# State-space scan chunks moved from beside the z projection into attention, with z through DRAM and the chunk results kept in SBUF

## The chip, the cores and the metric

The kernel runs on one core of a Trainium2 chip. The metric is the device time of one execution in microseconds (us). TensorE is PE in the profile's rows (PEld are its weight loads), VectorE is DVE, ScalarE is ACT, GpSimd is POOL and SyncE is SP. Each engine works through its own instructions in a fixed order; an instruction that waits holds up everything behind it on its engine. Loads are issued from SP's queue, nearly all stores from ACT's queue. L179 means line 179 of the kernel's file; after the change most line numbers behind 570 differ.

## The reference

Two layers over 256 context and 1024 latent tokens of width 1024. Each layer is a mixer and a SwiGLU feed-forward block, both with norms and a modulation. What matters here is the mixer's two halves, which share an input and an output projection:

```python
q, k, v, z, xbc, dt = split(h @ w_in)            # one projection
attn = softmax(q k^T / 8) v                      # 8 query heads, 2 key heads of 64
xs, B, C = split(silu(conv(xbc)))                # 8 state-space heads of 64, state 128
for direction in (forward, backward):            # chunks of 128 tokens
    scores  = (C B^T) * decay                    # inside a chunk
    y      += scores @ (xs*dt) + (C @ h_in) * exp(acum)   # h_in: state before the chunk
y   = rmsnorm((y + d_skip * xs) * silu(z)) * ssd_norm
out = concat(attn, y) @ w_out
```

Context tokens get an output in the first layer only, so layer 0 has ten tiles of 128 tokens in its mixer's output and layer 1 has eight. Context queries see the 256 context keys, latent queries all 1280.

## The kernel before, in words

Matmuls in reduced form (`fp32r`) take every operand as a high and a low part, and `mm3` (L177 to 181) does a product as three of them. `split` (L109 to 111) makes the two parts: ACT copies the high one, DVE (or POOL) subtracts to get the low one. A tile of 128 tokens is the unit of nearly everything.

A layer's mixer has these stages. The convolution's projection; `kv`; `q`, beside which `ssd_states` runs the state recurrence over the chunks and writes each chunk's incoming state `h_d` to DRAM; then `z`, and beside it the scan chunks; then attention with the output projection; then the feed-forward block. `w_tok` (L360) is the loop over tiles of the projections: 24 matmuls of 512 columns a tile for q and z, then the tile's evaluation, then a `filler`, which is one step of another stage's generator. This is how two stages are put beside each other: the order in which the program emits instructions sets priorities, and the framework's list scheduler then fixes each engine's order from it.

One scan chunk (`ssd`, L629) has three parts. `decays` builds a 128 x 1024 decay matrix for each direction: a select on POOL (L639), four broadcast matmuls (L644) and four scans on DVE (L648), and a sum on POOL (L649). `chunk` multiplies C with B (L664) and C with the states of both directions (L668), multiplies the decays with the first on DVE (L670) and multiplies that with the inputs (L674), eight heads of 64 columns. `finish` adds the parts (L681 to 685), multiplies with the gate (L686), norms (L688), transposes on PE (L691), splits, and stores the result to DRAM (`mix_d`, L694). Chunk inputs come from DRAM by three loads (L656 to 658). `gate` (L701) leaves silu(z) in one of eight small SBUF buffers (`s2`, 128 x 512). Four buffers `L` hold the decays of two chunks.

`attention` (L748) works in units of one tile, one key head and two of its query heads, four units a tile. `scores` multiplies q with k (L785), scales with the running minimum on DVE (L786), takes the exponential on ACT (L792), and normalizes on POOL (L794), into one of six probability buffers; it runs two units ahead of `values`, which transposes probabilities on PE (L807), splits them (L110, L111) into one of two, later three, buffers, and multiplies with v (L814). After the fourth unit of a tile `oproj` multiplies the tile before with `w_out` (48 matmuls of 512 columns); half of its input comes from attention, half is loaded again from `mix_d` (L833). `attention` is a generator, too: its first units run beside the last chunks, and it gets its third split buffer and the last two `w_out` tiles only when the chunks' memory is free (L1019). PSUM has five banks of kind `w` and three of kind `s`.

The pools that bind are `x` (six buffers of 128 x 1024: chunk inputs and states, q of even tiles, the output norm), `s2` (eight), `raw` (two: weights before the split, q of odd tiles) and a ring of five split weight tiles that `pump` fills in a planned order, z's units before `w_out`'s.

## Time and profile before

| | us |
|---|---|
| runs shown: median of 3 (lowest, highest) | 3388.87 (3368.36, 3391.09) |
| profiled execution: its own time | 3388.8 |
| its span, first to last instruction | 3387.1 |
| layer 0: first z matmul to first output projection | 343.3 to 554.9 |
| layer 0: steady attention, five tiles | 635.9 to 832.4 |
| layer 1: first z matmul to first output projection | 2149.6 to 2373.4 |
| layer 1: steady attention, four tiles | 2412.2 to 2569.3 |
| mean granted TensorE clock | 0.965 of full |

How to read it: the page gives busy time of each engine and, in 40 equal slices, its tenths; a busy PE includes time in which a matmul waits inside the engine's pipeline. A window's row gives the same for a stretch that the reader chooses, with the granted clock. A row in order of time begins with its start and its length; in square brackets stands how long the engine had been idle and what ended that. A group's row gives count, total busy time, mean ns of one, and idle time ahead of it by what ended it.

### The profile page before, as it was taken

Reading aid. Unit: us, or ns where it says so; the run is one execution under the profiler, and the core shown is the slowest. Engines: PE = TensorE matmul, PEld = TensorE weight load, DVE = VectorE, ACT = ScalarE, POOL = GpSimd, SP = SyncE. Lnnn points to the kernel's source line nnn. Section 1 sums busy time; section 2 is a strip of 40 time slices with the busy share of each in tenths; the row PEclk is TensorE's granted clock in tenths of the full one; section 3 lists DMA queues with packets and bytes.
Section 4 is the critical chain, followed back from the end, with each engine's and each line's share of the span. In section 5 each row is a group of like instructions: output and inputs, shape, how many; then the busy total and the mean of one; then the engine's idle time right before and its main releaser. Section 6 shows DMA issues by size and latency. Waiting matters only on the chain.

```text
span 3387.1 us, 44081 instructions
## 1 busy us (share of the span) xinstructions
PE 3151.0 (93%) x16599; PEld 2601.6 (77%) x16599; DVE 1833.4 (54%) x3298; ACT 1231.2 (36%) x2332; POOL 1364.4 (40%) x1267
## 2 busy tenths in 40 slices
PE   6899967999899999988999999887999999999997
PEld 4677656888777888876777788666888788888886
DVE  2557876666534334436334557887666344444446
ACT  4433236666632121134222343236666411111112
POOL 4327434544533223236344534744544421212213
PEclk8899888999999999999999999888999999999999
DMA  6276533211333222135444325632112311111113
GB/s 219 77 223 209 176 125 114 80 63 66 108 119 113 88 88 75 57 106 169 137 143 131 125 70 164 227 131 79 69 69 82 100 49 45 57 38 56 45 49 112
DMA packets 283981, 360.00 MB, mean 106 GB/s; under 512 B 18160, under 2 KB 212176, under 8 KB 283512
## 3 DMA queue, kind: packets, MB, share of 16 engines
q1 hardware_dynamic: 237768, 291.71, 27.5%
q10 hardware_dynamic: 46000, 65.47, 5.3%
q8 instruction: 131, 2.15, 0.3%
q14 instruction: 82, 0.67, 0.1%
HBM read 291.61 MB, written 65.52 MB: 105 GB/s over the span
## 4 chain that ended last, share of the span: by engine, by line
PE 43%; DVE 3%; DMA 3%; POOL 2%; issue 2%; ACT 1%; ACTq 0%; POOLq 0%; DVEq 0%; SPq 0%
PE ps_w L179 7%; PE ps_w L180 7%; PE ps_w L181 7%; PE ps_s L179 4%; PE ps_s L181 4%; PE ps_s L180 4%; PE ps_w L814 2%; PE ps_w L807 2%; PE ps_s L785 2%; DMA xt<-in_norm_mix_post 1%; POOL w_t L111 1%; PE ps_w L230 0%; DVE xt L411 0%; POOL rstd_t L187 0%; DMA raw_t<-in_w_in 0%
## 5 line engine op out<-in xcount | busy, mean ns | idle before, releaser
L111 POOL TENSOR_TENSOR w_t<-raw_t,w_t 128x1024 fp32r<-128x1024 f32 (+1 forms) x220 | 546.7, 2488 | 1238.9 <-ACT w_t L110 1230.0
L929 DVE TENSOR_TENSOR ffn_acc<-ffn_acc,ps_s 128x512 f32<-128x512 f32 x560 | 380.2, 686 | 371.5 <-PE ps_s L181 369.7
L110 ACT CAST w_t<-raw_t 128x1024 fp32r<-128x1024 f32 (+1 forms) x248 | 256.7, 1037 | 669.4 <-PE ps_w L181 233.7
L179 PE MATMUL ps_s<-w_t,xt 128*128 128x512 f32 x792 | 315.0, 398 | 18.8 <-DVE ffn_acc L929 7.7
L181 PE MATMUL ps_s<-w_t,xt 128*128 128x512 f32 x792 | 308.8, 392 | 2.5 <-DVE xt L111 2.5
L180 PE MATMUL ps_s<-w_t,xt 128*128 128x512 f32 x792 | 310.0, 391 | 0.0
L910 DVE TENSOR_TENSOR s2t<-s2t,ps_w 128x512 f32<-128x512 f32 (+1 forms) x110 | 69.7, 634 | 439.9 <-PE ps_w L181 439.7
L786 DVE TENSOR_SCALAR_CACHE_REDUCE att_a<-ps_s 128x512 f32<-128x512 f32 (+1 forms) x400 | 227.4, 587 | 144.4 <-PE ps_s L785 131.1
L179 PE MATMUL ps_w<-hb,w_t 128*128 128x512 f32 x704 | 276.4, 393 | 3.5 <-ACT s2t L333 2.6
L179 PE MATMUL ps_w<-ha,w_t 128*128 128x512 f32 x704 | 275.0, 392 | 1.8 <-POOL ha L337 1.8
L181 PE MATMUL ps_w<-hb,w_t 128*128 128x512 f32 x704 | 275.5, 391 | 0.0
L180 PE MATMUL ps_w<-hb,w_t 128*128 128x512 f32 x704 | 275.3, 391 | 0.0
L180 PE MATMUL ps_w<-ha,w_t 128*128 128x512 f32 x704 | 275.2, 391 | 0.0
L181 PE MATMUL ps_w<-ha,w_t 128*128 128x512 f32 x704 | 274.9, 391 | 0.0
L794 POOL TENSOR_SCALAR att_a<-att_a,att_st 128x1280 f32<-128x1280 f32 (+1 forms) x144 | 181.8, 1265 | 163.2 <-DVE att_st L793 93.1
L110 ACT CAST xt<-s2t 128x512 fp32r<-128x512 f32 (+2 forms) x148 | 80.4, 543 | 423.4 <-DVE s2t L910 351.9
L807 PE MATMUL ps_w<-cst_all,att_a 128*128 128x128 f32 x1312 | 199.7, 278 | 0.8 <-issue 0.8
L792 ACT ACTIVATE att_a<-att_a,att_st 128x1280 f32<-128x1280 f32 (+1 forms) x144 | 183.0, 1272 | 36.5 <-DVE att_st L791 29.4
L179 PEld LDWEIGHTS ps_s<-w_t,xt 128*128 128x128 f32 x792 | 149.4, 189 | 60.5 <-issue 9.7
L111 DVE TENSOR_TENSOR xt<-s2t,xt 128x512 fp32r<-128x512 f32 (+2 forms) x148 | 167.9, 1134 | 39.3 <-ACT xt L110 37.5
L181 PEld LDWEIGHTS ps_s<-w_t,xt 128*128 128x128 f32 x792 | 148.8, 188 | 36.7 <-DVE xt L111 3.8
L180 PEld LDWEIGHTS ps_s<-w_t,xt 128*128 128x128 f32 x792 | 149.6, 189 | 26.5 <-issue 0.4
(268 smaller groups left out, 7338.3 us busy)
## 6 DMA issues: line engine op xcount, KB each, us to landing
raw_m<-in_w_mod SPq DMA_DIRECT2D x80, 512.0 KB
raw_t<-in_w_gate SPq DMA_DIRECT2D x66, 512.0 KB
raw_t<-in_w_up SPq DMA_DIRECT2D x66, 512.0 KB
raw_t<-in_w_down SPq DMA_DIRECT2D x66, 512.0 KB
xt<-xs SPq DMA_DIRECT2D x44, 512.0 KB
raw_t<-in_w_in SPq DMA_DIRECT2D x32, 512.0 KB
xs<-xt ACTq DMA_DIRECT2D x28, 512.0 KB
ssd_x<-xtok SPq DMA_DIRECT2D x36, 384.0 KB
```

The lines of the kernel that those rows point to most:

```text
L110: self.nc.scalar.copy(hi, src)
L111: (eng or self.nc.vector).tensor_tensor(lo, src, hi.bitcast(F32), op=ALU.subtract)
L179: mm(out, st[0], mv[0], start=first, stop=False)
L180: mm(out, st[0], mv[1], start=False, stop=False)
L181: mm(out, st[1], mv[0], start=False, stop=last)
L785: nc.tensor.matmul(s[:, :m], qs[t][c][:, hd], kst[:, g, j:j + m], start=c == 0, stop=c == 1)
L786: nc.vector.tensor_scalar(pb[:, j:j + m], s[:, :m], -0.125, None, op0=ALU.mult, op1=ALU.min, accum_out=st[:, n:n + 1])
L792: nc.scalar.activation(pb, pb, AF.Exp, bias=nmx, scale=-1.0, accum_out=st[:, 4:5])
L794: nc.gpsimd.tensor_scalar(pb, pb, st[:, 5:6], 1.0, op0=ALU.mult, op1=ALU.mult)
L807: nc.tensor.transpose(tp[:, (2 * k + h) * P:(2 * k + h + 1) * P], pr[h][:, (k2 + k) * P:(k2 + k + 1) * P], self.ident)
L910: nc.vector.tensor_tensor(s, s, ps["u"][:, :n], op=ALU.mult)
L929: nc.vector.tensor_tensor(acc[t][:, s], acc[t][:, s], p, op=ALU.add)
```

## The change

The z stage no longer has a filler. `gate` sends silu(z) to a new DRAM tensor `z_d`, and `mix_d` is gone. The scan is driven from the loop over attention's units: three steps a tile, one after each of the first three units, so that chunk t is computed in the units of tile t (`chunk`; load and decays of the next; `finish`). Its result stays as two `s2` buffers (`mix`) until `oproj` of that tile, at the end of the next tile. There is one pair of decay buffers, of which one lies in attention's large buffer `ha`, so that five probability buffers are left; `scores` is called for one head before and one head after `values`. The three split buffers and all of `w_out` are laid out from the start; the last three `w_out` tiles are loaded at the beginning of attention. The additions in `chunk` and `finish` are ordered so that PSUM is left earlier. The constant masks are loaded where `ssd_prep` needs them instead of at the program's start, and the state recurrence has a pool of its own that closes before z.

```diff
-        c = self.cst.tile([P, 6 * P + 2 * NT], F32, name="cst_all")
...
+        c = self.cst.tile([P, P + 2 * NT], F32, name="cst_id")
...
-        self.mix_d = [d(f"mix{l}", [NT, P, 1024]) for l in range(DEPTH)]
+        self.z_d = [d(f"z{l}", [NT, P, 512]) for l in range(DEPTH)]
...
+        mk = self.x(n=5 * P)
+        nc.sync.dma_start(mk, self.I["cst"][:, P:6 * P])
...
+    def gate(self, l, t, p):
+        z = self.s2()
+        self.nc.scalar.activation(z, p, AF.Silu)
+        self.nc.scalar.dma_start(self.z_d[l][t], z)
...
+        def load(c):
+            bx, hin, z = self.x(), self.x().rearrange("p (d n) -> p d n", d=2), self.s2()
...
+            nc.sync.dma_start(z, self.z_d[l][c])
+            ins[c] = bc, hin, xt, z
...
-            L = [lp.tile([P, 1024], F32, tag="L", bufs=4, name="ssd_L") for d in range(2)]
...
-            pi = [self.psw(), self.psw()]
+            ys = []
             for d in range(2):
+                pi = self.psw()
                 for g in range(2):
...
+                y = self.s2()
+                nc.vector.tensor_tensor(v8(y), v8(pi), hb8(self.ex[:, 0, d, c]), op=ALU.mult)
+                ys.append(y)
...
             nc.vector.tensor_tensor(y2, y2, y, op=ALU.add)
+            nc.vector.tensor_tensor(y2, y2, py, op=ALU.add)
+            mid[c] = y, y2, xt, z
...
-            self.split(y2.bitcast(F32R), y.bitcast(F32R), pt)
-            for i, half in enumerate((y2, y)):
-                nc.scalar.dma_start(self.mix_d[l][c, :, i * 512:(i + 1) * 512], half)
...
+            hi, lo = self.s2(F32R), self.s2(F32R)
+            self.split(hi, lo, pt)
+            mix[c] = hi, lo
...
         def steps():
-            for i in range(len(cs) + 1):
...
+            load(cs[0])
+            decays(cs[0])
+            yield
+            for i, c in enumerate(cs):
+                chunk(c)
+                yield
                 if i + 1 < len(cs):
...
+                    load(cs[i + 1])
+                    decays(cs[i + 1])
                 yield
...
+                finish(c)
+                yield
...
-        pbuf = [ha[:, i * TOK:(i + 1) * TOK] for i in range(6)]
+        NPB = 5
+        pbuf = [ha[:, i * TOK:(i + 1) * TOK] for i in range(NPB)]
...
+        L = [lp.tile([P, 1024], F32, name="ssd_L"), ha[:, NPB * TOK:NPB * TOK + 1024]]
+        mix = {}
+        scan = self.ssd(l, L, ha[:, NPB * TOK + 1024:NPB * TOK + 1536], mix)
...
-            ms = self.x()
-            nc.sync.dma_start(ms, self.mix_d[l][t])
-            ms = ms.bitcast(F32R).rearrange("p (s k n) -> p k s n", s=2, k=4)
+            hi, lo = (a.rearrange("p (k n) -> p k n", k=4) for a in mix.pop(t))
...
+        next(scan)
         for i, u in enumerate(units):
             if i + 2 < len(units):
-                scores(units[i + 2])
+                scores(units[i + 2], (0,))
...
             values(u)
...
-            if i % 4 == 3 and i > 3:
+            if i + 2 < len(units):
+                scores(units[i + 2], (1,))
+            if i % 4 < 3:
+                next(scan, None)
+            elif i > 3:
                 oproj(tiles[i // 4 - 1])
...
-                k.w_tok(l, "z", 512, qt, gate, zfill)
-                att = k.attention(l, early)
...
+                k.w_tok(l, "z", 512, qt, lambda t, p: k.gate(l, t, p), lambda: k.load_q(l, qt[0]) if next(nz) == len(qt) - 3 else None)
...
+                with tc.tile_pool(name=f"att{l}", bufs=1, reuse_waits="tile") as atp:
+                    k.attention(l, kv, atp, early)
```

What this does to the engines' orders shows in three places. PE within layer 0's z stage, before (L179 to L181 are z, the rest a scan chunk):

```order
L180 MATMUL ps_s<-w_t,ha 128x512
L181 MATMUL ps_s<-w_t,ha 128x512
L668 MATMUL ps_w<-xt 128x256 x4
L179 MATMUL ps_s<-w_t,ha 128x512
L180 MATMUL ps_s<-w_t,ha 128x512
L181 MATMUL ps_s<-w_t,ha 128x512
L674 MATMUL ps_w<-xt,ssd_L 128x64 x8
L179 MATMUL ps_s<-w_t,ha 128x512
L180 MATMUL ps_s<-w_t,ha 128x512
L181 MATMUL ps_s<-w_t,ha 128x512
L664 MATMUL ps_s<-xt 128x128 x2
```

PE at the end of layer 0's z stage, now (L809 are scores, L830 transposes, L837 values; L661, L673, L678 are the decays' and the chunk's matmuls):

```order
L179 MATMUL ps_s<-w_t,hb 128x512
L180 MATMUL ps_s<-w_t,hb 128x512
L181 MATMUL ps_s<-w_t,hb 128x512
L809 MATMUL ps_s<-att_c,xt 128x256 x4
L661 MATMUL ps_w<-eaT,pick 128x512 x4
L809 MATMUL ps_s<-att_c,xt 128x256 x8
L673 MATMUL ps_s<-xt 128x128 x2
L809 MATMUL ps_s<-att_c,xt 128x256 x2
L830 MATMUL ps_w<-cst_id,att_a 128x128 x4
L809 MATMUL ps_s<-att_c,xt 128x256 x2
L837 MATMUL ps_w<-att_c,att_b 128x256
L678 MATMUL ps_w<-xt 128x256 x4
```

Here z's matmuls end in one run, 179 of them without another instruction between, and the first chunk stands behind the first scores.

DVE in a steady tile of layer 0's attention, before (L786 are score evictions, L111 splits, L791 and L793 the softmax's small steps):

```order
L793 RECIPROCAL att_st<-att_st 128x1
L786 TENSOR_SCALAR att_a,att_st<-ps_s 128x512
L111 TENSOR_TENSOR att_pt<-ps_w,att_pt 128x512
L111 TENSOR_TENSOR att_b<-ps_w,att_b 128x512
L786 TENSOR_SCALAR att_a,att_st<-ps_s 128x256
L111 TENSOR_TENSOR att_c<-ps_w,att_c 128x512
L786 TENSOR_SCALAR att_a,att_st<-ps_s 128x512 x2
```

And now (L810 are the evictions; L665 the scans, L698 the gate's product, L700 the norm):

```order
L665 SCALAR_TENSOR_TENSOR ssd_L<-ps_w,ssd_L 128x512
L810 TENSOR_SCALAR att_a,att_st<-ps_s 128x512
L111 TENSOR_TENSOR att_c<-ps_w,att_c 128x512
L665 SCALAR_TENSOR_TENSOR ssd_L<-ps_w,ssd_L 128x512
L810 TENSOR_SCALAR att_a,att_st<-ps_s 128x256
L698 TENSOR_TENSOR s2t<-s2t 128x512
L815 TENSOR_REDUCE att_st<-att_st 128x1
L665 SCALAR_TENSOR_TENSOR att_a<-ps_w,att_a 128x512 x2
L815 TENSOR_REDUCE att_st<-att_st 128x1
L111 TENSOR_TENSOR att_pt<-ps_w,att_pt 128x512
L810 TENSOR_SCALAR att_a,att_st<-ps_s 128x512
L700 SCALAR_TENSOR_TENSOR s2t<-s2t,rstd_t,att_a 128x512
```

The chunk's DVE work now stands between the evictions and splits that PE waits for.

SP's queue around the load of v in layer 0, now (L121 and L780 are `w_out` tiles, L768 is v, L651 z, L751 q, L648 a chunk's B and C):

```order
L640 DMA att_a<-in_ssd_norm 128x512
L121 DMA raw_t<-in_w_out 128x1024 x2
L768 DMA att_b<-v_108 128x10x256
L651 DMA s2t<-z_114 128x512
L780 DMA raw_t<-in_w_out 128x1024 x2
L751 DMA xt<-q_104 128x1x1024 x2
L780 DMA raw_t<-in_w_out 128x1024
L648 DMA xt<-bc_102 128x4x128
```

Before, v stood behind chunk inputs and two `w_out` tiles and ahead of q; the last three `w_out` tiles came much later. The DRAM name is the one the program gives.

More of the change, by code (lines that the diff above doesn't have):

```diff
@@ L572, in ssd_prep @@
         p = ps()
-        for i, m in enumerate((self.m_le, self.m_ge, self.m_gt, self.m_lt, self.ones, self.ones)):
-            nc.tensor.matmul(p[:, i * n:(i + 1) * n], m, u[:, (i % 2) * n:(i % 2 + 1) * n], start=True, stop=True)
+        mk = self.x(n=5 * P)
+        nc.sync.dma_start(mk, self.I["cst"][:, P:6 * P])
+        for i, m in enumerate((0, 2, 1, 3, 4, 4)):
+            nc.tensor.matmul(p[:, i * n:(i + 1) * n], mk[:, m * P:(m + 1) * P], u[:, (i % 2) * n:(i % 2 + 1) * n], start=True, stop=True)
         nc.scalar.activation(exf, p[:, 0:6 * n], AF.Exp)
@@ L746, in load_q, with attention @@
             self.qs[t].append(q.bitcast(F32R).rearrange("p (h n) -> p h n", h=NH))
-    def attention(self, l, early=None):
+    def attention(self, l, lp, atp, early=None):
         nc = self.nc
@@ L757, in attention @@
         mxa = [hbv(2560 + i * 1024, 1024).rearrange("p (k s n) -> p k s n", k=4, s=2) for i in range(2)]
-        ptb = [hbv(4608, 1024), hc[:, 3072:4096]]
-        wob = [hbv(5632, 2048)]
+        apt = atp.tile([P, 1024], F32R, name="att_pt")
+        ptb = [(hc[:, 3072:3584], hc[:, 3584:4096]), (apt[:, 0:512], apt[:, 512:1024]), (hc[:, 2560:3072], hbv(7680, 512))]
         nc.sync.dma_start(kst.bitcast(F32), self.k_d[l])
         nc.sync.dma_start(vst.rearrange("p t g n -> p t (g n)").bitcast(F32), self.v_d[l].rearrange("t p n -> p t n"))
+        wo = {}
+        for kt in range(self.RING):
+            u = self.U[l, "o", kt]
+            wo[kt] = [(u[:, 0, 0, n * 512:(n + 1) * 512], u[:, 1, 0, n * 512:(n + 1) * 512]) for n in range(2)]
+        halves = lambda w: [(w[:, n * 512:(n + 1) * 512], w[:, 1024 + n * 512:1536 + n * 512]) for n in range(2)]
+        wo[5] = halves(hbv(4608, 2048))
+        wo[6] = halves(atp.tile([P, 2048], F32R, name="att_wo"))
+        w7 = atp.tile([P, 1024], F32R, name="att_wo7")
+        wo[7] = [(w7[:, 0:512], w7[:, 512:1024]), (hbv(6656, 512), hbv(7168, 512))]
+        for kt in range(self.RING, KT):
+            r = self.raw.tile([P, 1024], F32, tag="raw", name="raw_t")
+            nc.sync.dma_start(r, self.I["w_out"][l][kt * P:(kt + 1) * P, :])
+            for n in range(2):
+                self.split(*wo[kt][n], r[:, n * 512:(n + 1) * 512])
+        L = [lp.tile([P, 1024], F32, name="ssd_L"), ha[:, NPB * TOK:NPB * TOK + 1024]]
+        mix = {}
+        scan = self.ssd(l, L, ha[:, NPB * TOK + 1024:NPB * TOK + 1536], mix)
         count = {"p": 0, "t": 0}
@@ L765, in attention, with scores @@
         qs, prs = self.qs, {}
-        def scores(u):
+        def scores(u, heads=(0, 1)):
             t, g, hp = u
@@ L771, in scores @@
                 self.load_q(l, t)
-            if g == 0 and hp == 1 and t + 1 < NT:
+            if g == 0 and hp == 1 and t + 1 < NT and 0 in heads:
                 self.load_q(l, t + 1)
-            pr = []
-            for h in range(2):
+            pr = prs.setdefault(u, [])
+            for h in heads:
                 hd = 4 * g + 2 * hp + h
-                pb = pbuf[count["p"] % 6][:, :nk]
+                pb = pbuf[count["p"] % NPB][:, :nk]
                 count["p"] += 1
@@ L813, in values @@
                         kt = k2 + k
-                        nc.tensor.matmul(av, vst[:, kt, g], pt[:, c, k * 256:(k + 1) * 256], start=kt == 0 and c == 0,
+                        nc.tensor.matmul(av, vst[:, kt, g], pt[c][:, k * 256:(k + 1) * 256], start=kt == 0 and c == 0,
                                          stop=kt == nk - 1 and c == 1)
@@ L851, in attention @@
             scores(u)
-        wo = [self.U[l, "o", kt] for kt in range(self.RING)]
-        atp = yield
+        next(scan)
         for i, u in enumerate(units):
             if i + 2 < len(units):
-                scores(units[i + 2])
+                scores(units[i + 2], (0,))
             if early and i == len(units) - 1:
@@ L859, in attention @@
             values(u)
-            if atp is None:
-                atp = yield
-                if atp:
-                    ptb.append(atp.tile([P, 1024], F32R, name="att_pt"))
-                    wob += [atp.tile([P, 2048], F32R, tag="wo", bufs=2, name="att_wo") for _ in range(2)]
-                    for kt, dst in zip(range(self.RING, KT), wob):
-                        src = self.I["w_out"][l][kt * P:(kt + 1) * P, :]
-                        wo.append(self.unit([(slice(0, 1024), src.unsqueeze(1))], (1, 1024), dst.rearrange("p (s n) -> p s n", s=2)))
-            if i % 4 == 3 and i > 3:
+            if i + 2 < len(units):
[3 more added lines that the diff above has]
+            elif i > 3:
                 oproj(tiles[i // 4 - 1])
```

92 lines of the change are left out of this document (31 added, 61 removed).

## The prediction

> **What bounds the kernel now.** I read the page first, then the busy time by stage, then the order of events on TensorE (PE) between the z projection and the first output projection, then instruction groups for prices.
>
> ```profile
> span 3387.1 us, 44081 instructions
> PE 3151.0 (93%) x16599; PEld 2601.6 (77%) x16599; DVE 1833.4 (54%) x3298; ACT 1231.2 (36%) x2332; POOL 1364.4 (40%) x1267
> PE   6899967999899999988999999887999999999997
> PEclk8899888999999999999999999888999999999999
> ```
>
> PE is busy 93% of the span, so a gain has to come out of the stages where it is not, or where its granted clock is low: here the slices that read 6 and 7 (423 to 593 us, layer 0) and 8, 8, 7 (2117 to 2371 us, layer 1). There the busy time by stage is, in rows of window, PE, PEld, VectorE (DVE), ScalarE, GpSimd (POOL), clock, DMA share, GB/s:
>
> ```profile
> 343.34:554.85 211.51, 159.25 (x737) 124.73 (x736) 152.78 (x222) 78.19 (x205) 93.15 (x97) 0.81 0.43 145
> 2149.56:2373.40 223.84, 183.41 (x951) 147.47 (x950) 179.38 (x328) 100.22 (x214) 109.63 (x98) 0.89 0.38 129
> 635.86:832.35 196.49, 196.48 (x1283) 174.84 (x1282) 137.17 (x431) 134.38 (x261) 96.43 (x120) 1.00 0.20 72
> 2412.16:2569.33 157.17, 157.16 (x1026) 139.88 (x1025) 109.73 (x345) 107.50 (x209) 77.21 (x96) 1.00 0.19 68
> 375.11:438.32 63.21, 63.13 (x319) 49.53 (x318) 55.70 (x59) 19.10 (x60) 29.76 (x27) 1.00 0.42 138
> 460.00:480.00 20.00, 14.78 (x65) 11.31 (x65) 14.31 (x15) 8.28 (x17) 5.01 (x5) 0.83 0.57 177
> ```
>
> The first two windows run from the first z matmul of a layer to its first output projection, the "head" below. PE idles 52.3 us in the one and 40.4 us in the other, at clocks of 0.81 and 0.89. The next two hold five and four tiles of steady attention: 39.3 us a tile, PE never idle, DVE busy 27.4 us of it. The fifth holds five rounds of "a z tile and a scan chunk": 12.64 us a round, DVE busy 11.1 us.
>
> ```profile
> 343.34 0.39 PE L179 MATMUL ps_s<-w_t,hc 128*128 128x512 f32 x1
> 380.45 0.40 PE L179 MATMUL ps_s<-w_t,ha 128*128 128x512 f32 x1
> 383.67 0.39 PE L181 MATMUL ps_s<-w_t,ha 128*128 128x512 f32 x1
> 463.00 1.19 PE L664 MATMUL ps_s<-xt 128*128 128x128 f32 x4 [7.75 <-DMA xt<-bc]
> 506.35 0.58 PE L785 MATMUL ps_s<-att_c,raw_q 128*128 128x256 f32 x1 [10.72 <-DMA raw_q<-q]
> 532.63 0.58 PE L814 MATMUL ps_w<-att_c,att_b 128*128 128x256 f32 x1 [6.91 <-ACT att_c L110]
> 554.85 0.40 PE L179 MATMUL ps_w<-w_t,att_b 128*128 128x512 f32 x1
> 2149.56 0.39 PE L179 MATMUL ps_s<-w_t,ha 128*128 128x512 f32 x1
> 2156.07 0.56 PE L179 MATMUL ps_s<-w_t,ha 128*128 128x512 f32 x1 [2.26 <-ACT w_t L110]
> 2373.40 0.48 PE L179 MATMUL ps_w<-w_t,att_b 128*128 128x512 f32 x1
> ```
>
> These are PE's first z matmul, two z matmuls 14 starts apart (3.22 us, so 0.23 us each), three waits, and the first output projection at 554.85; then the same ends for layer 1. The waits are of a scan that shares PE's fixed order with z and then with attention's start: chunk inputs late by 7.75 us, q by 10.72, an eviction by 6.91.
>
> **The change, its head.** z becomes 24 matmuls a tile with nothing between. Layer 0: 240 x 0.23 = 55.2 us from 343.3; the wait for the last weight unit stays (2.3 us in layer 1's row), as do the last q transposes and a few slow matmuls after a stall, say 6 us in all. z ends near 405. Layer 1: 192 x 0.23 = 44.2 from 2149.6, ending near 2202 with 8 us for the same. Then attention must reach its first output projection, two tiles of units plus two chunks away, and here DVE has more to do than PE:
>
> ```profile
> L786 DVE TENSOR_SCALAR_CACHE_REDUCE att_a<-ps_s 128x512 f32<-128x512 f32 x256 | 172.9, 683 | 119.7 <-PE ps_s L785 110.3 <-PE ps_w L807 9.2
> L786 DVE TENSOR_SCALAR_CACHE_REDUCE att_a<-ps_s 128x256 f32<-128x256 f32 x144 | 59.5, 416 | 24.7 <-PE ps_s L785 20.7 <-PE ps_w L807 4.0
> L786 DVE DVE_READ_ACCUMULATOR att_a<-ps_s 128x1 f32 x400 | 33.0, 83 | 0.0
> L791 DVE TENSOR_REDUCE att_st<-att_st 128x1 f32<-128x3 f32 x128 | 18.9, 148 | 0.6
> L793 DVE RECIPROCAL att_st<-att_st 128x1 f32<-128x1 f32 x144 | 22.6, 158 | 31.0 <-ACT att_a L792 30.8
> L111 DVE TENSOR_TENSOR att_pt<-ps_w,att_pt 128x512 fp32r<-128x512 f32 x106 | 72.4, 683 | 4.7 <-ACT att_pt L110 4.6
> L111 DVE TENSOR_TENSOR w_t<-raw_t,w_t 128x1024 fp32r<-128x1024 f32 x28 | 37.5, 1343 | 15.0 <-ACT w_t L110 15.0
> 478.63 2.33 DVE L648 TENSOR_TENSOR_SCAN ssd_L<-ps_w,ssd_L 128x512 f32<-128x512 f32 x2
> L648 DVE TENSOR_TENSOR_SCAN ssd_L<-ps_w,ssd_L 128x512 f32<-128x512 f32 x72 | 84.2, 1206 | 9.5 <-PE ps_w L644 9.5
> ```
>
> Two scans together take 2.33 us where each takes 1.206: neighbours overlap by 0.08 us, which I take off sums of single rows. Layer 0: a context unit costs DVE 2 x (0.416 + 0.083 + 0.158) + 0.683 = 2.0, eight of them 16; the scores of the first two latent units run ahead, four heads of 2 x 0.683 + 0.416 + 3 x 0.083 + 0.148 + 0.158 = 2.34, so 9.4; two chunks 22.2; seven w_out tiles to split at 1.343, 9.4. Sum 57, less 0.08 for some hundred rows: 49. I add 11 us for the start: v (1280 KB, 7.2 us at the 177 GB/s of the window at 460) can load only after z has freed its buffer, with two w_out tiles ahead of it in SyncE's queue and z, w_out and q behind it; PE's first value matmul waits for it, and the chunk's own matmuls stand behind that one. First output projection near 465 instead of 554.9: **90 us earlier**. Layer 1: eight latent units at 27.4/4 = 6.85 are 55, with 9.4, 22.2 and 9.4 that is 96, less 2.4 of overlap in the sums of single rows, and 5 for the part of the start that the scores don't cover: near 2300 instead of 2373.4, **73 us earlier**. Together 163.
>
> **The change, its tail.** Those chunks that the head no longer holds, 8 of 10 in layer 0 and 6 of 8 in layer 1, now lie in steady tiles, where PE has no idle time to give. What does one add to 39.3 us? From below: its PE time, a round's 12.64 less 24 x 0.23 = 5.5, so 7.1 us with the cost of changing between matmul shapes. From above: its DVE time, 11.1 us, if none hides. By sums over a whole tile DVE has room (27.4 + 11.1 = 38.5 of 46.4 us), but not in every stretch. In the new DVE order the chunk's work lies in a run of some thirty rows, W product to norm, with seven splits, ten score evictions (seven wide, three narrow) and six small ones between. Attention's part there is 14 x 0.683 + 3 x 0.416 + 10 x 0.083 + 6 x 0.15 = 12.5, less 0.08 x 28 = 10.3; the chunk's is 11.1 less its last split, 10.5. Together 20.8 us. PE beside it has 7 of a tile's 20 transpose blocks (39.3 less 48 x 0.23 for the output projection, less eight heads' scores at 5 x 0.23, over 20: 0.95 us each, 6.7), 17 x 0.23 = 3.9 us of scores and the chunk's 7.1: 17.7. So PE falls behind by 3.1 us there, and buffers (five w banks in PSUM, three split buffers) let it recover somewhat more than half. I take **7.1 + 1.4 = 8.5 us** a tile, nearer the lower end: PE was full at a DVE share of 88% in the round of z and scan, too. 14 x 8.5 = 119.
>
> **Put at nothing.** z goes out and comes back (256 KB each way) where mix did with 512 KB: under z's matmuls out, a unit or more ahead in; uncovered, 1.8 us a tile at 145 GB/s, 32 in all. The masks load later (320 KB, 2.3 us a layer at that rate) beside the long DVE polynomial that feeds the same matmuls. Five probability buffers for six: the second head's scores now follow the values of two units before, and lie under the next unit's transposes; were that cover gone, DVE would set the pace, which is rival B. The mix reload leaves SyncE's queue at no gain, since steady PE never waits for it.
>
> **Sum.** The durations are of the profiled execution, 3388.8 us with a span of 3387.1; the median of the runs is 3388.87, the same within 0.1. 3388.8 - 163 + 119 = 3344.8, so **3345 us**, 1.3% less. As a cross-check, 163 less the 14 x 7.1 = 99 of PE work that moves out is 64, below the 92.7 us that PE idles in both heads. With 7.5 to 9.5 us a tile this case runs from 3331 to 3359.
>
> **Rivals.**
> A, PE hides all: a chunk adds only its 7.1 us, 3388.8 - 163 + 99 = 3325; for it, DVE's sum of 38.5 in 46.4; against, the crowded stretch. With every wait of the start gone as well (11 + 5 us there, 6 + 8 in z), 3295.
> B, DVE sets the tile: 11.1 us each, 155 given back, 3381. For it, DVE is in order, and attention's splits that PE waits for queue behind 1.2 us scans; against, PE was full at 88% of DVE.
> C, slower: DVE and POOL block each other. The chunk's three DVE operations with both inputs in SBUF vary as no PSUM reader does (minimum, median, maximum in ns):
>
> ```profile
> L681 DVE TENSOR_TENSOR s2t<-s2t x18: 672/1235/1868, 376.0 to 2287.0; 128x512 f32<-128x512 f32 x18
> L686 DVE TENSOR_TENSOR s2t<-s2t x18: 673/692/2448, 384.6 to 2292.8; 128x512 f32<-128x512 f32 x18
> L688 DVE SCALAR_TENSOR_TENSOR s2t<-s2t,rstd_t,ssd_nrm x18: 726/752/2485, 390.3 to 2298.2; 128x512 f32<-128x512 f32 x18
> L794 POOL TENSOR_SCALAR att_a<-att_a,att_st 128x1280 f32<-128x1280 f32 x128 | 173.2, 1354 | 161.2 <-DVE att_st L793 91.3 <-PE ps_w L807 40.8 <-PE ps_s L785 27.1
> ```
>
> Among the 1.354 us probability scalings of attention, eight a tile, each may wait for a whole one: medians of 2.7 together would become 2.1 + 4.1 = 6.2, 3.5 us more. With B's exposure that is 14.6 a tile, 204 given back: 3430. It decides from 163/14 = 11.6 us a tile on. Against it, the medians of two of the three are near their minima already with POOL at 47% in that window. The Trainium skill (SBUF — State Buffer, section "Who interferes with whom") speaks for it: a VectorE instruction with two SBUF inputs and a GpSimd instruction that reads SBUF exclude each other for the whole instruction. The maxima of the three rows agree with that; the medians say how seldom it is paid here.
> D, the head isn't gained in full: z's end releases some 9 MB of loads before the first output projection (v, five w_out tiles, three q tiles, chunk inputs), 62 us at 145 GB/s, as long as DVE's sum. If they follow each other badly, as the 10.72 us wait for q shows, 20 us a layer are lost: 3385, and the change hardly does what it says.
>
> **How the numbers follow.** Forecast 0.38, A 0.22, B 0.17, C 0.11, D 0.12. A measurement of this kernel can tell about 1% (34 us) from no change. Faster by more: all of A, 0.28 of the forecast's 0.38, 0.03 each of B and D: 0.56. Slower: C, 0.02 of B, 0.01 of D: 0.14. Within: 0.30. The range reaches from the best of A to 3410, beyond B and D; most of C is left out: 3295 to 3410.
>
> **What would show it.** The first output projections near 465 and, with all later times shifted by layer 0's gain, 73 us earlier after layer 1's first z matmul; z tiles 5.5 us apart; steady tiles of 47.8 us with DVE near 80%. Tiles over 51 us prove the tail wrong, a head shortened by less than 60 us in layer 0 proves the start wrong, and PE waiting in steady tiles for anything but DVE's splits and evictions proves the mechanism wrong.

## The result, and the profile after

The change made the kernel slower. The forecast was 3345 us, 1.3% faster, with a range of 3295 to 3410; the result lies outside it and on the other side.

| | before | after |
|---|---|---|
| median of the runs, us | 3386.3 | 3484.6 |
| lowest and highest | 3368.4, 3391.1 | 3475.0, 3486.4 |
| ratio, 95% interval | | 1.0295 (1.0252 to 1.0337) |
| first output projection, layer 0 and layer 1 | 554.9, 2373.4 | 507.9, 2379.4 |
| steady attention tile, us | 39.3 | 53.3 |

The page of the profiled execution after (3475.0 us) opens with the span, the busy times, and PE and its granted clock in 40 slices:

```profile
span 3473.3 us, 43952 instructions
PE 3198.2 (92%) x16599; PEld 2610.0 (75%) x16599; DVE 1837.6 (53%) x3304; ACT 1229.0 (35%) x2336; POOL 1353.2 (39%) x1267
PE   6999659999999999998999999979999999999997
PEclk8999769999999999999999999989999999999999
```

Work hardly changed (DVE 4 us more in all), yet the span grew by 86.2 us. The places are found from the output projections: first z matmul and first projection of each layer after, then the ninth projection of layer 0 and the seventh of layer 1.

```profile
326.26 0.39 PE L179 MATMUL ps_s<-w_t,hc 128*128 128x512 f32 x1
507.85 0.63 PE L179 MATMUL ps_w<-w_t,att_b 128*128 128x512 f32 x1
928.47 0.39 PE L179 MATMUL ps_w<-w_t,att_b 128*128 128x512 f32 x1
2207.49 0.39 PE L179 MATMUL ps_s<-w_t,ha 128*128 128x512 f32 x1
2379.41 0.40 PE L179 MATMUL ps_w<-w_t,att_b 128*128 128x512 f32 x1
2692.19 0.39 PE L179 MATMUL ps_w<-w_t,att_b 128*128 128x512 f32 x1
```

Before, the ninth and the seventh stood at 868.49 and 2605.52:

```profile
868.49 0.40 PE L179 MATMUL ps_w<-w_t,att_b 128*128 128x512 f32 x1
2605.52 0.39 PE L179 MATMUL ps_w<-w_t,att_b 128*128 128x512 f32 x1
```

The heads gained 554.85 - 507.85 = 47.0 us in layer 0, and 223.8 - (2379.41 - 2207.49) = 51.9 in layer 1: 98.9 where the forecast has 163. Even that flatters the change. 17.1 of the 47.0 us were gained ahead of z, for which the forecast has nothing: PE's waits for the modulation's weights (`raw_m`) add up to 12.8 us before and 1.5 after, but to 11.8 to 14.4 in nine of the eleven variants of the changed kernel below, so most of this seems to belong to the one execution that was profiled, 10 us faster than the median. From first projection to last of these, layer 0 takes 420.6 instead of 313.6 us and layer 1 312.8 instead of 232.1: the tails give back 107.0 + 80.7 = 187.7, where the forecast has 119. The balance, 88.8 us slower, is the span's 86.2 within 3. So the tails missed by 69 us and the heads by 64.

**The tail, cut at the projection.** A steady tile has two stretches: the output projection (48 matmuls), and the rest. Before, and after (two tiles that alternate); columns as in the forecast's windows, window and length, PE, PEld, DVE, ACT, POOL, clock, DMA share, GB/s:

```profile
635.86:648.37 12.51, 12.51 (x62) 10.48 (x61) 2.37 (x9) 4.28 (x10) 4.49 (x6) 1.00 0.13 53
648.37:675.14 26.77, 26.77 (x197) 24.50 (x197) 25.06 (x78) 22.59 (x43) 14.80 (x18) 1.00 0.29 102
```

```profile
722.85:734.85 12.00, 12.00 (x59) 9.96 (x58) 2.91 (x12) 4.53 (x10) 4.04 (x5) 1.00 0.01 1
734.85:774.64 39.79, 36.50 (x229) 30.48 (x228) 35.42 (x84) 24.69 (x54) 22.27 (x25) 0.96 0.26 86
774.64:787.10 12.46, 12.46 (x62) 10.49 (x61) 2.79 (x9) 3.73 (x8) 2.71 (x4) 1.00 0.01 2
787.10:829.21 42.11, 38.05 (x241) 30.47 (x241) 37.21 (x93) 26.80 (x56) 23.76 (x26) 1.00 0.23 82
```

This is the view that the prediction lacked. Before, DVE looks 70% busy over a tile (27.4 of 39.3), but it is 94% busy in the rest (25.06 of 26.77) and idle through most of the projection. After, it still does only 2.8 us in the projection, and all of the chunk's work has gone into the rest: 36.3 us on average, in a stretch of 41.0 (over four tiles). DVE's own timeline shows the idle projection; the bracket is idle time and what ended it:

```profile
621.58 0.17 DVE L817 RECIPROCAL att_st<-att_st 128x1 f32<-128x1 f32 x1 [1.18 <-ACT att_a L816]
629.50 0.69 DVE L111 TENSOR_TENSOR att_c<-ps_w,att_c 128x512 fp32r<-128x512 f32 x1 [7.76 <-ACT att_c L110]
```

**The head of layer 0.** z itself ran as forecast: its last gating ends at 390.1, 64 us after the first matmul. From there the first projection is another 118 us off, not 60. PE's waits in that stretch:

```profile
438.63 1.01 PE L809 MATMUL ps_s<-att_c,raw_q 128*128 128x256 f32 x3 [27.45 <-DMA raw_q<-q]
450.64 1.01 PE L809 MATMUL ps_s<-att_c,raw_q 128*128 128x256 f32 x3 [7.97 <-DMA raw_q<-q]
457.91 1.09 PE L703 MATMUL ps_w<-cst_id,s2t 128*128 128x128 f32 x4 [4.34 <-DVE s2t L700]
495.44 1.65 PE L809 MATMUL ps_s<-att_c,xt 128*128 128x512 f32 x4 [13.66 <-DVE att_a L810]
504.49 1.12 PE L703 MATMUL ps_w<-cst_id,s2t 128*128 128x128 f32 x4 [4.97 <-DVE s2t L700]
```

The largest is q of the second tile (`raw_q`), 35.4 us in two pieces. SyncE's DMA queue shows where that q stood:

```profile
398.64 1.59 SPq L780 DMA_DIRECT2D raw_t<-in_w_out  x2
401.87 1.05 SPq L751 DMA_DIRECT2D xt<-q  x2
405.30 6.09 SPq L780 DMA_DIRECT2D raw_t<-in_w_out  x1
411.49 1.00 SPq L648 DMA_DIRECT2D xt<-bc  x1
412.59 6.24 SPq L751 DMA_DIRECT2D raw_q<-q  x1
418.89 6.11 SPq L650 DMA_DIRECT2D xt<-xtok  x1
425.05 0.42 SPq L651 DMA_DIRECT2D s2t<-z  x1
431.69 0.51 SPq L751 DMA_DIRECT2D raw_q<-q  x1
```

It shares two raw buffers with rows 5 to 7 of `w_out`, and the second half of it is issued at 431.69, behind loads for the chunk. It also stands behind the third tile's q (`xt<-q`, issued at 401.87), which PE first uses at 465.31.

The 13.66 us at 495.44 are a late load as well, two engines away:

```profile
488.68 2.34 POOL L731 TENSOR_TENSOR gate_row<-gate_row,xt 128x1024 f32<-128x1024 f32 x1 [18.26 <-DMA xt<-in_norm_mix_post]
493.79 0.93 DVE L698 TENSOR_TENSOR s2t<-s2t 128x512 f32<-128x512 f32 x1 [13.32 <-POOL s2t L697]
```

POOL waited for the weights of the norm behind the output projection (`norm_mix_post`), which SyncE issued at 465.69, behind the fourth tile's q. The chunk's sum stood behind that on POOL, the gate product behind the sum on DVE, and the score evictions that PE needed behind the gate product.

### The profile page after: what moved, and what is told of

Read it like the earlier page. It is cut to its first block, busy times and chain, and to the rows that moved or that the text cites. A ratio compares the mean times of both kernels' runs of the same rounds, so it can differ in the third digit from the quotient of the medians.

```text
span 3473.3 us, 43952 instructions
## 1 busy us (share of the span) xinstructions
PE 3198.2 (92%) x16599; PEld 2610.0 (75%) x16599; DVE 1837.6 (53%) x3304; ACT 1229.0 (35%) x2336; POOL 1353.2 (39%) x1267
## 4 chain that ended last, share of the span: by engine, by line
PE 39%; DVE 6%; DMA 2%; POOL 2%; issue 2%; ACT 1%; SPq 0%; ACTq 0%; POOLq 0%; DVEq 0%
PE ps_w L179 7%; PE ps_w L181 7%; PE ps_w L180 7%; PE ps_s L179 4%; PE ps_s L181 4%; PE ps_s L180 4%; PE ps_w L837 2%; PE ps_s L809 2%; DVE att_a L810 1%; PE ps_w L830 1%; POOL w_t L111 1%; DMA raw_q<-q 1%; DMA xt<-xtok 1%; DVE s2t L700 0%; POOL rstd_t L187 0%
## 5 line engine op out<-in xcount | busy, mean ns | idle before, releaser
L111 POOL TENSOR_TENSOR w_t<-raw_t,w_t 128x1024 fp32r<-128x1024 f32 (+1 forms) x220 | 534.8, 2434 | 1223.0 <-ACT w_t L110 1222.6
L179 PE MATMUL ps_s<-w_t,xt 128*128 128x512 f32 x792 | 314.5, 397 | 18.2 <-DVE ffn_acc L945 7.9
L181 PE MATMUL ps_s<-w_t,xt 128*128 128x512 f32 x792 | 308.3, 391 | 2.3 <-DVE xt L111 2.3
L810 DVE TENSOR_SCALAR_CACHE_REDUCE att_a<-ps_s 128x512 f32<-128x512 f32 (+1 forms) x400 | 229.1, 584 | 109.3 <-PE ps_s L809 99.4
L179 PE MATMUL ps_w<-hb,w_t 128*128 128x512 f32 x704 | 277.2, 394 | 1.4 <-POOL hb L337 0.9
L179 PE MATMUL ps_w<-ha,w_t 128*128 128x512 f32 x704 | 275.0, 392 | 1.4 <-POOL ha L337 1.4
L181 PE MATMUL ps_w<-hb,w_t 128*128 128x512 f32 x704 | 276.0, 392 | 0.0
L181 PE MATMUL ps_w<-ha,w_t 128*128 128x512 f32 x704 | 274.8, 391 | 0.0
L830 PE MATMUL ps_w<-cst_id,att_a 128*128 128x128 f32 x1312 | 198.3, 280 | 8.9 <-POOL att_a L818 2.8
L179 PEld LDWEIGHTS ps_s<-w_t,xt 128*128 128x128 f32 x792 | 149.0, 188 | 59.7 <-issue 13.1
L111 DVE TENSOR_TENSOR xt<-s2t,xt 128x512 fp32r<-128x512 f32 (+2 forms) x148 | 167.9, 1134 | 40.9 <-ACT xt L110 40.5
L809 PE MATMUL ps_s<-att_c,raw_q 128*128 128x512 f32 (+1 forms) x400 | 124.2, 420 | 63.5 <-DMA raw_q<-q 42.7
L181 PEld LDWEIGHTS ps_s<-w_t,xt 128*128 128x128 f32 x792 | 148.6, 188 | 36.3 <-DVE xt L111 3.5
```

Source lines behind the costliest of these rows:

```text
L111: (eng or self.nc.vector).tensor_tensor(lo, src, hi.bitcast(F32), op=ALU.subtract)
L179: mm(out, st[0], mv[0], start=first, stop=False)
L181: mm(out, st[1], mv[0], start=False, stop=last)
L809: nc.tensor.matmul(s[:, :m], qs[t][c][:, hd], kst[:, g, j:j + m], start=c == 0, stop=c == 1)
L810: nc.vector.tensor_scalar(pb[:, j:j + m], s[:, :m], -0.125, None, op0=ALU.mult, op1=ALU.min, accum_out=st[:, n:n + 1])
L830: nc.tensor.transpose(tp[:, (2 * k + h) * P:(2 * k + h + 1) * P], pr[h][:, (k2 + k) * P:(k2 + k + 1) * P], self.ident)
```

## The experiments

Two theories were set against each other for the tail. **Stage by stage**: the projection gives DVE no work, the rest of the tile is where DVE's work counts, so what the tile costs follows DVE's work in the rest. The rivals: **fewer buffers** (five probability buffers, heads of a unit apart), **PE** (its own added matmuls and queue), and **blocking** between DVE and POOL. For the head: **queue order** against **bandwidth**.

### The buffers alone

The kernel before, with this part of the change and nothing else:

```diff
-        pbuf = [ha[:, i * TOK:(i + 1) * TOK] for i in range(6)]
+        pbuf = [ha[:, i * TOK:(i + 1) * TOK] for i in range(5)]
...
-                scores(units[i + 2])
+                scores(units[i + 2], (0,))
...
             values(u)
+            if i + 2 < len(units):
+                scores(units[i + 2], (1,))
```

> The kernel before with one part of the change alone: five probability buffers instead of six, and the second head's scores of a unit issued behind the values of the running unit. The chunks stay beside z. Theory (stage by stage): the steady tile stays at 39.3 us within 0.4 us, time 3380 to 3395 against 3386. Rival (fewer buffers): of the 14.0 us that a tile grew by, the 2.4 to 2.9 that exceed DVE's added 11.1 to 11.9 are this part, so the tile is about 41.9 and the time 3420 or more (14 tiles or more times 2.4).

Measured 3384.5 us against 3384.6 (ratio 1.0002, 0.9987 to 1.0018). A projection and the rest behind it:

```profile
669.50:682.00 12.50, 12.50 (x63) 10.53 (x62) 2.98 (x9) 3.96 (x9) 3.38 (x6) 1.00 0.01 2
682.00:709.10 27.10, 27.10 (x198) 24.67 (x198) 25.10 (x78) 22.64 (x44) 16.13 (x19) 1.00 0.18 68
```

39.6 us, PE never idle: this part costs nothing on its own. Whether a sixth buffer would help beside the chunks wasn't tried: it does not fit in `ha`, where the second decay buffer and the norm's weights lie now.

### More PE work, more DVE work, less DVE work

Three copies of the changed kernel, each with one engine's work altered:

```diff
-                nc.tensor.matmul(py[:, h * HD:(h + 1) * HD], W[:, h * P:(h + 1) * P], xt[:, h * HD:(h + 1) * HD], start=True, stop=True)
+                for _ in range(2):
+                    nc.tensor.matmul(py[:, h * HD:(h + 1) * HD], W[:, h * P:(h + 1) * P], xt[:, h * HD:(h + 1) * HD], start=True, stop=True)
```

> The changed kernel with the W times x matmuls of every chunk issued twice (the second writes the same values): 1.9 us more of PE a tile, nothing more of DVE, ACT or POOL. Theory (DVE sets a steady tile outside the projection): they fall into the 3.4 to 4.1 us a tile in which PE waits there, tile up to 0.6 longer, 3485 to 3494. Rival (PE's own queue sets it): 1.9 us more in each of 14 tiles and in the head, 3511 to 3521.

```diff
-                nc.vector.tensor_tensor(v8(y), v8(pi), hb8(self.ex[:, 0, d, c]), op=ALU.mult)
+                for _ in range(2):
+                    nc.vector.tensor_tensor(v8(y), v8(pi), hb8(self.ex[:, 0, d, c]), op=ALU.mult)
```

> The changed kernel with the two evictions of C times states of every chunk issued twice (same values): 1.36 us more of DVE a tile, nothing more of PE, ACT or POOL. Theory (DVE sets a steady tile outside the projection, at 0.88 busy): 1.4 to 1.6 us a tile, in 14 tiles and a little in the heads, 3504 to 3512. Rival (PE's own queue sets it): under 0.4 us a tile, 3485 to 3491.

```diff
-                    nc.vector.tensor_tensor_scan(Lh, ea, Lh, 0.0, op0=ALU.mult, op1=ALU.add)
+                    if False:
+                        nc.vector.tensor_tensor_scan(Lh, ea, Lh, 0.0, op0=ALU.mult, op1=ALU.add)
```

> The changed kernel with the four scans of every chunk's decays left out (the decay matrix then holds only the selected step sizes, so the state-space half of the output is not the reference's); the four matmuls, all buffers and all other work stay. 4.83 us less of DVE a tile, PE's work as it was. Theory (outside the projection the tile takes DVE's work there plus some 4 us of handing over): 4.5 to 5.5 us a tile, in 14 tiles and a little in the heads, 3402 to 3425. Rival (the stalls are those of the order and of PE's own queue, 37 us of PE busy in that stretch): at most the 1.7 us a tile that a mere change of order gave in the run with more PE work, 3455 to 3490.

Measured: more PE work 3447.9 us (1.0180, 1.0153 to 1.0207), more DVE work 3491.2 (1.0309, 1.0284 to 1.0333), no scans 3435.3 (1.0144, 1.0131 to 1.0157). The rest of a tile in the three, one fence each (the last has two kinds of tile, as the changed kernel has):

```profile
721.26:760.44 39.18, 37.05 (x250) 31.88 (x248) 35.27 (x88) 25.35 (x54) 21.93 (x24) 1.00 0.26 88
```

```profile
697.12:738.24 41.12, 35.80 (x234) 29.72 (x232) 37.43 (x88) 24.97 (x53) 22.24 (x25) 1.00 0.24 84
```

```profile
679.96:715.95 35.99, 34.36 (x230) 29.27 (x228) 30.44 (x80) 24.58 (x54) 22.19 (x25) 1.00 0.27 95
728.40:767.37 38.97, 36.48 (x243) 30.59 (x242) 32.43 (x89) 26.82 (x56) 23.54 (x26) 1.00 0.26 88
```

More PE work made the tile shorter, 51.6 us, and so met neither expectation: the program's instruction scheduler, given other work, wrote another order, in which DVE does 35.3 us in the rest instead of 36.3 and idles 3.9 instead of 4.7. So it isn't the amount of PE's work that sets the tile, though the run doesn't hold PE's order fixed. The order is worth 1.7 us a tile or more, and the second run added only 1.36 of DVE work. It lengthened the tile by 0.4: its time is outside its theory's 3504 to 3512 and at the edge of its rival's 3485 to 3491, and against such a difference between orders it decides little. The third has the larger step: 4.83 us less DVE work, tile 49.7, so 3.6 us less, between the two expectations. DVE's work is most of the cause and not all of it. Without the scans PE is busy 34.4 of 36.0 and 36.5 of 39.0 us in the rest: its own work is 26.8 as before and 7.2 in the chunk's five groups of matmuls, 34.0 us, so it is likely to be the next bound.

### Moving chunk work to the projection

First the decays alone, ahead of the projection (the edit shown), then the finish too, with one more step of the scan behind `oproj`:

```diff
                 if i + 1 < len(cs):
                     load(cs[i + 1])
-                    decays(cs[i + 1])
                 yield
                 finish(c)
                 yield
+                if i + 1 < len(cs):
+                    decays(cs[i + 1])
+                yield
...
-            if i % 4 < 3:
-                next(scan, None)
-            elif i > 3:
+            next(scan, None)
+            if i % 4 == 3 and i > 3:
                 oproj(tiles[i // 4 - 1])
```

> The decays of the next chunk (four matmuls, four scans, 4.8 us of DVE) go from the second unit of a tile to the fourth, ahead of the output projection. Theory (stage by stage): in the changed kernel a steady tile is 12.2 us of output projection, in which DVE works 2.8 us, and 41.1 us of the rest, in which it works 36.3; only the rest is set by DVE, and the whole chunk was put there. Every us of scans that comes to lie under the projection then takes about 1.1 us off the tile: 2.7 us if half of the scans land there, 5.5 if all do, so a tile of 47.8 to 50.6 us and a time of 3408 to 3447 us against 3484.6. Rival (fewer buffers: five probability buffers, heads of a unit issued apart): the work is the same and so are the buffers, tile within 1 us of 53.3, time over 3470. Rival (blocking between DVE and POOL): same, since the long norm instruction stays where it is, over 3470. The forecast's own reading (a tile's DVE total against its PE total) expects no change, 3485.

> As the run before it, and the finish of a chunk (gate product, norm, hi and lo split: 3.5 us of DVE, 2.1 of them the norm) goes behind the output projection of the fourth unit too, so that 8.3 us of 11.9 are there. Theory: the rest of the tile then has 28 to 30 us of DVE, less than PE's 31.5 to 33 (26.8 before, plus the 7.2 of the chunk less the decays' 1.6), so PE sets it: tile 44.5 to 47 us, time 3484.6 less 14 times 6.3 to 8.8, that is 3361 to 3397. Rival (fewer buffers): what buffers cost stays, tile over 51, time over 3450. If the chunk tile of 8.5 us in the forecast was possible at all, this order should come near it (39.3 + 8.5 = 47.8).

Measured 3435.3 us (1.0145, 1.0107 to 1.0183) and 3502.5 (1.0351, 1.0324 to 1.0377): the first where the theory put it, the second on the wrong side of both kernels. A projection and a rest of the first, and DVE at that projection's start:

```profile
772.20:783.50 11.30, 11.30 (x51) 9.23 (x51) 3.23 (x7) 4.06 (x9) 7.41 (x7) 1.00 0.00 0
783.50:822.00 38.50, 37.29 (x245) 31.30 (x243) 34.51 (x92) 25.74 (x55) 18.36 (x23) 1.00 0.26 90
```

```profile
772.88 2.32 DVE L665 TENSOR_TENSOR_SCAN att_a<-ps_w,att_a 128x512 f32<-128x512 f32 x2
```

The tile is 49.8 us, as expected for half of the scans, and two of the four do lie in the projection. (The expectation of the next version says that all were over by its start; that is wrong.) But DVE's work there rose only from 2.8 to 3.2 us, since evictions and splits that had reached into the projection's start now lie ahead of it. So the gain isn't simply the two scans: it is 1.8 us less DVE work in the rest (1.15 of it in the norm, below), 0.7 less idle, and a projection 0.9 shorter. In the second, DVE reached the projection's evictions first and stood there:

```profile
735.08 1.41 DVE L744 SCALAR_TENSOR_TENSOR xt<-ps_w,rstd_t,gate_row 128x512 f32<-128x512 f32 x2 [10.35 <-POOL rstd_t L187]
```

DVE takes its instructions in order. L744 scales the projection's own result and waits for its norm, so the finish's norm and split, which stood behind it, could not start for 10.35 us, and then came on top of the next tile's evictions: tile 55.4. This lies in the range of the rival (fewer buffers, over 51 and over 3450), but the wait is for a norm, not for a buffer.

A third version spreads the decays through the projection, so that PE's order forces all four scans into it; a fourth adds the later `w_out` loads of the next section:

```diff
                 for n in range(2):
                     for kt in range(KT):
+                        if fill and kt % 4 == 0:
+                            fill()
                         one(n, kt)
```

> The four matmul and scan pairs of the next chunk's decays are spread over the output projection, one ahead of every twelve of its 48 matmuls, so that the scans cannot be done before it. (When the decays were only put ahead of the projection, the tile fell to 49.8 us, but DVE still worked only 3.3 us in the projection's 11.3: the scans had been done by its start.) Theory (the stretch outside the projection is set by DVE): three or four scans of 1.2 us leave that stretch, its DVE work falls from 34.5 to 30 to 31 us, at the same share of 0.9 it takes 33 to 34.5, the projection 12.8: tile 46 to 47.5 us, time 3435 less 14 times 2.3 to 3.8, that is 3382 to 3403. Rival (PE sets that stretch by now: 37.4 of 38.6 us busy there): the decays' 1.5 us of matmuls only change places, tile 49.3 to 49.8, time over 3425.

> The spread decays together with the later loads of w_out rows 5 to 7. Theory: both gains add, since one is in the steady tiles and one in the heads: the time of the spread decays less 30 to 39 us, 3345 to 3373. Rival: the heads then wait for something else (the second context tile's chunk, in layer 0 still bound by what lands at 170 GB/s), less than 15 us of the 39 are kept.

Measured 3457.4 us (1.0213, 1.0188 to 1.0237) and 3421.5 (1.0107, 1.0086 to 1.0128). Both miss their theory's total, and the first lies in its rival's (over 3425); the step between them, 35.9 us, is the 30 to 39 expected.

```profile
678.24:714.36 36.12, 34.40 (x234) 29.19 (x231) 31.37 (x85) 25.47 (x54) 21.54 (x25) 1.00 0.27 95
714.36:728.31 13.95, 13.95 (x61) 10.65 (x61) 7.16 (x16) 4.42 (x9) 4.07 (x6) 1.00 0.01 3
728.31:766.82 38.51, 34.73 (x237) 29.93 (x235) 32.89 (x88) 25.63 (x54) 22.08 (x25) 1.00 0.27 88
```

Here DVE does 6.2 to 7.2 us in the projection and 32.1 on average in the rest, where the theory had 30 to 31. But the rest takes 37.3, not 33 to 34.5, and the projection grew to 14.0: 51.3 a tile, longer than the rival's 49.3 to 49.8, too, with PE busy 34.4 to 34.7 us of the rest. The idle 5 us of DVE in the rest did not go away with its work.

### The head: w_out later

```diff
-        for kt in range(self.RING, KT):
+        def load_wo(kt):
             r = self.raw.tile([P, 1024], F32, tag="raw", name="raw_t")
...
+            if 0 < i < 4:
+                load_wo(self.RING + i - 1)
```

> Only the loads and splits of rows 5 to 7 of w_out move, from ahead of the first scores to behind the second, third and fourth unit of a layer. Theory (order in SP's queue and the two raw buffers): q of tile 1 then no longer stands behind three weight loads, PE's waits of 27.5 and 8.0 us for raw_q in layer 0 go down to under 10 together, the first output projection of layer 0 starts near 480 us instead of 507.9, time 3445 to 3465. Rival (bandwidth): the same bytes have to land before the first projection at the 145 to 170 GB/s seen there, the first projection stays within 8 us of 507.9 and the time over 3475. The steady tiles stay at 53.3 us in either.

Measured 3445.3 us (1.0185, 1.0163 to 1.0206), on the theory's edge. PE's waits for q, and the first projection of layer 0:

```profile
423.02 0.38 PE L810 MATMUL ps_s<-att_c,raw_q 128*128 128x256 f32 x1 [2.89 <-DMA raw_q<-q]
433.12 1.01 PE L810 MATMUL ps_s<-att_c,raw_q 128*128 128x256 f32 x3 [9.71 <-DMA raw_q<-q]
489.30 0.63 PE L179 MATMUL ps_w<-w_t,att_b 128*128 128x512 f32 x1
```

The DMA in the middle of these waits; SyncE had issued nothing but q from 403 to 429:

```profile
420.00:430.00 10.00, 0.52 (x3) 0.19 (x1) 0.43 (x2) 1.47 (x5) 2.17 (x4) 0.69 0.13 52
```

35.4 us of waiting became 12.6, not the under 10 expected, and the projection came 18.6 us earlier although z ended 11.8 us later, behind 13.4 us of waits for `raw_m` instead of 1.5: the start took 87 us, not 118. Queue order was 30 us of the miss. Of these, 22.8 are q's, and 11.2 are in PE's waits for score evictions (19.9 before, 8.7 now), since the weights of `norm_mix_post` now stood ahead of the fourth tile's q; other waits grew a little. The three `w_out` rows still landed ahead of that projection, so the bandwidth of all loads was not the cause. The rate of a q load is part of what remains: alone, q moved 52 GB/s at a DMA share of 0.13, the work of two engines in sixteen, so 512 KB take some 10 us (an estimate from that row). The forecast had priced its loads at 145 to 177 GB/s. Why q moves so slowly no run tests; the program writes such a load as 2 x 64 x 1024. Some 27 us over the forecast's 60 remain, in which PE waits for q (12.6), for DVE's norm (10.5 in two pieces) and for score evictions.

### Together, and two further steps

The decays ahead of the projection with the later `w_out` loads; then the same with two SBUF-only operations on POOL; then, without that, the finish cut in three (sum; gate product and norm; transposes and split) and issued later:

> Decays ahead of the projection and w_out rows 5 to 7 loaded later, together. Theory: the two gains (49 and 39 us) add, one in the tiles and one in the heads: 3390 to 3402, ratio to before 1.001 to 1.005, no longer told apart from it by 1%. Rival: they overlap, since a head that starts its tiles earlier meets the tiles' own rate, 3410 to 3425.

```diff
-            nc.vector.tensor_tensor(y2, y2, y, op=ALU.add)
+            nc.gpsimd.tensor_tensor(y2, y2, y, op=ALU.add)
...
-            nc.vector.tensor_tensor(y, y, z, op=ALU.mult)
+            nc.gpsimd.tensor_tensor(y, y, z, op=ALU.mult)
```

> Decays ahead of the projection, w_out rows 5 to 7 loaded later, and two SBUF-only operations of each chunk (the sum of the two state terms and the gate product, 0.68 us each) from DVE to POOL, where they take about 1.28 each and POOL is half idle. Theory (DVE's work sets the tile): 1.36 us less of DVE a tile than in the same kernel without that move, 1.2 to 1.6 us a tile, 17 to 24 us less, 3372 to 3382 if that one takes 3396. Rival (POOL and DVE block each other in SBUF): POOL's 2.6 us more a tile hold up DVE's SBUF operations (the norm, the step from scores to reciprocals) and the chain of POOL's scaling to the transposes, no gain or a loss of up to 1 us a tile, 3392 to 3410.

```diff
             for i, c in enumerate(cs):
+                if i:
+                    finish_split(cs[i - 1])
                 chunk(c)
...
-                finish(c)
+                finish_sum(c)
                 yield
+                finish_norm(c)
```

> The two changes together (decays ahead of the projection, w_out rows 5 to 7 later), with the finish of a chunk cut in three: the sum with the skip term in the third unit, gate product and norm at the head of the fourth, transposes and the hi and lo split in the next tile's first. Same work, same buffers; the question is whether the 3 to 5 us a tile in which DVE idles outside the projection belong to the order. Theory (DVE's work and PE's, both near 34 us, set that stretch, and some 4 us of handing over stay in any order): tile 49 to 50.5 us, time 3383 to 3402 beside the 3392 of the two together. Rival (the idle time is the order's, and a chunk cut finer gives DVE work where it idles): tile 47 to 48.5 us, 3355 to 3380, which would be faster than the kernel before.

Measured 3392.3 us (1.0016, 1.0006 to 1.0026), 3401.7 (1.0049, 1.0036 to 1.0062) and 3395.3 (1.0026, 1.0013 to 1.0039). The two gains add, and bring the changed kernel back to the time of the kernel before, not below it. POOL's help shortened the tile by 0.9 us (48.9), less than the 1.36 that left DVE, and with another order in the heads the total was 9 us worse: its theory's 3372 to 3382 is missed, its rival's 3392 to 3410 met, but not by the tile. The finer finish gave 50.7 us a tile, just over its theory's 49 to 50.5: the rival that all of DVE's idle time belonged to the order got no support.

## Why the prediction was wrong, point by point

**The tail is the step that failed**: "7.1 + 1.4 = 8.5 us a tile", and with it the upper bound, "its DVE time, 11.1 us, if none hides". A chunk cost 14.0 us in a full steady tile (53.3 - 39.3), 13.4 on the mean of all fourteen. By stretches:

| us a tile | before | after | difference |
|---|---|---|---|
| projection | 12.5 | 12.2 | -0.3 |
| rest: DVE busy | 25.1 | 36.3 | +11.2 |
| rest: DVE idle | 1.7 | 4.7 | +3.0 |

The prediction did notice that DVE's room was not in every stretch, and then priced only one crowded run of thirty rows and let buffers "recover somewhat more than half" of it. But there was nothing to recover in: outside the projection DVE was at 94% before the change, and no chunk work was placed in the projection. So all of DVE's work added to the tile, which is rival B's price. The bound was broken because it took DVE as fully busy, and DVE idles 3.0 us more of the rest than before. That PE (34.0 us of work) and DVE (36.3), nearly equal, wait for each other there fits this, but it is argued and not shown.

The sizes over all variants, in us:

| kernel | tile | rest | DVE busy in rest | idle |
|---|---|---|---|---|
| before | 39.3 | 26.8 | 25.1 | 1.7 |
| no scans | 49.7 | 37.5 | 31.4 | 6.1 |
| decays spread | 51.3 | 37.3 | 32.1 | 5.2 |
| ahead, w_out later, POOL | 48.9 | 37.6 | 33.5 | 4.1 |
| decays ahead | 49.8 | 38.5 | 34.5 | 4.0 |
| finish in three | 50.7 | 39.5 | 34.6 | 4.9 |
| more PE work | 51.6 | 39.2 | 35.3 | 3.9 |
| changed | 53.3 | 41.0 | 36.3 | 4.7 |
| more DVE work | 53.7 | 41.1 | 37.4 | 3.7 |
| finish behind the projection | 55.4 | 44.2 | 36.3 | 7.9 |

With chunks in it, the rest is DVE's work plus 4 to 6 us, and 7.9 where the order is bad. **What stays open** is what those 4 to 6 us are made of. Fewer buffers cost nothing without chunks, and more PE work came with a shorter tile, though in another order; part is the order that the scheduler writes (1.7 us from one order to another). The rest of it no run isolates: the PSUM banks, for one, no run varied.

**The head** failed in its start, "I add 11 us for the start". z was right (64 us for 62; its end came at 390 and not 405 because it began 17 us earlier, most of that, it seems, by luck of the profiled execution), and DVE's sum too: 17.9 + 8.0 + 20.0 + 7.4 = 53 us busy between 390 and 508 against 49. The time without DVE work was not: 65 us, not 11. The prediction named v as what comes late; it was q of the second tile, behind `w_out` rows that are needed last and behind the third tile's q, and after it the weights of `norm_mix_post`, behind the fourth tile's. Rival D had the cause (loads that follow each other badly) but 20 us a layer for 43 and 21, and the run with `w_out` later shows that 30 us in layer 0 were order. In layer 1 PE's wait for q is 7.3 us; there DVE did 95.5 us of work in a start of 115.9, and what makes up the other 20 no run isolates.

**What was right**: the buffers and split heads at nothing (measured alone, without chunks), z through DRAM under z's matmuls, the 7.1 us of PE work (7.2), and PE's waits in steady tiles, which are DVE's evictions and the splits on ACT and DVE, as the forecast's last test asked.

**Rival C** came near in number (14.6 a tile) and not in mechanism. Of the three operations that were to be blocked, two stayed at their minima; the third, the norm, did not (minimum, median, maximum in ns):

```profile
L689 DVE TENSOR_TENSOR s2t<-s2t x18: 665/685/1247, 430.1 to 2674.2; 128x512 f32<-128x512 f32 x18
L698 DVE TENSOR_TENSOR s2t<-s2t x18: 676/682/928, 454.1 to 2678.8; 128x512 f32<-128x512 f32 x18
L700 DVE SCALAR_TENSOR_TENSOR s2t<-s2t,rstd_t,att_a x18: 743/1848/2850, 457.0 to 2684.0; 128x512 f32<-128x512 f32 x18
```

That is 1.4 us a tile in the steady stretch (2.13 against 0.74), not 3.5, and it is within DVE's 36.3.

## What to carry to other kernels

Cut the profile at the stages before asking where an engine has room: 70% over a tile was 94% in the part where the new work would land, and idle in the part where the order put none. An upper bound that adds one engine's work is only an upper bound if that engine is never made to wait; where two engines come within a few per cent of each other, allow some tenth of the stretch for handing over. When work moves into a stage that starts on loads, write down the DMA queue in its new order, ask of each load who waits for it first, and take its rate from a row in which it is alone.
